# GpSimd makes twelve of the weights' low halves in a two-layer decoder trunk

## The chip, the cores and the metric

The kernel runs on one core of a Trainium2 chip. The metric is the device time of one execution in microseconds (us). The time before is the median of three runs. All times of instructions come from one profiled execution of the kernel before.

## What is computed

A decoder trunk of two layers on one sequence of 256 tokens with 1024 features, in float32:

```python
def reference(x, ...):
    h = x
    for i in range(DEPTH):                       # 2 layers
        hn = rmsnorm(h, mix_norm_g[i])
        if i % N_MIXERS == 0:
            mix = gated_deltanet(hn, ...)        # layer 0, 8 heads of 128, chunkwise delta rule
        else:
            mix = moba_layer(hn, ...)            # layer 1, block attention with ALiBi
        h = h + mix.astype(h.dtype)
        h = h + squared_relu_mlp(rmsnorm(h, mlp_norm_g[i]), mlp_w_up[i], mlp_w_down[i])
    return rmsnorm(h, final_norm_g)
```

The work is mostly products of the 256 tokens with weight matrices: 1024x4112 into the DeltaNet mixer and 1024x1024 out of it, 1024x3072 and 1024x1024 for the attention, and 1024x4096 and back for each of the two MLPs.

## The kernel before

All large weights are laid out by the host as a stream of 200 units. A unit is a tile of 128x1024 float32 (512 KB) and is used once, in order. To keep float32 accuracy on TensorE (PE) each float32 value is split into a high half that is rounded to the type float32r and a low half that is the rest, and a product is made of three matmuls: high times high, high times low, low times high (`mm3`, lines 128 to 133; `natural` and `mlp_last` write out the same three).

`prep(u)` (lines 105 to 117) prepares one unit. SyncE (SP) issues its DMA from HBM into `wf`, which has three buffers (line 114). ScalarE (ACT) copies `wf` to `wh`, which rounds (line 115). VectorE (DVE) subtracts, `wl = wf - wh` (line 116). `wh` and `wl` have five buffers each. The first eight units (`WHALF = 8`) go in two pieces of 512 columns each, the others in one. `unit()` (lines 121 to 126) hands out the next unit and first prepares all units up to four ahead (`LEAD = 4`).

Units 0 to 31 belong to the DeltaNet projections: 16 units for the q/k pairs of eight heads (`pair`, PSUM tile `ps_kq`), 8 for v (`ps_v`) and 8 for z (`natural`, `ps_z`), in the order of the string `ORDER`. Units 32 to 39 are the mixer's output projection (`ps_g`), and from unit 40 on follows the first MLP (`ps_up_m`, then `ps_dn_m`), the attention (`ps_qk`, `ps_vn`, `ps_a`) and the second MLP (`ps_up_m`, `ps_last`).

In the DeltaNet part VectorE has much beside L116: it scales each projection into `cin` (L478), adds three taps of the short convolution (L484, six per pair, from the SBUF tiles `cin` and `y`), multiplies the tanh form of silu (L510, `kq`, followed by PE's transposes `kqt` of L517), prepares the decay (L463, `ms`), scales the k and q products (L549, `ua`, from PSUM) and inverts the triangular matrices (L569 to L642). GpSimd only fills tiles with zeros: `cin` (L472), `xt` (L564) and `xy` (L565).

The kernel is written with Tile: the semaphores are put in by it, and the order on each engine is made by a planner that can depart from the order of the source. Each engine then runs its own instructions strictly in that order.

Of the kernel before, what the change touches and what calls it, by code (L numbers as in the profile page):

```python
# [7 lines left out]
F32 = mybir.dt.float32  # L8
# [17 lines left out]
LEAD = 4  # L26
WHALF = 8
WARM = 6
NLAST = 2
NTANH = 3  # L30
RS = 3.0 / 8
# [44 lines left out]
def trunk_kernel(ctx: ExitStack, tc: tile.TileContext, xT, wst, wba, par, con, selc, gfin, out):  # L76
    nc = tc.nc
# [8 lines left out]
    def bank(role, shape, name):  # L86
        tag = ROLE[role]
        return psum.tile(shape, F32, tag=tag, name=name, bufs=BANKS[tag])
# [16 lines left out]
    def prep(u):  # L105
        if u >= NUNIT or u in ring:
            return
        wf = wpool.tile([P, CW], F32, tag="wf", name=f"wf{u}", bufs=3)
        wh = wpool.tile([P, CW], F32R, tag="wh", name=f"wh{u}")
        wl = wpool.tile([P, CW], F32R, tag="wl", name=f"wl{u}")  # L110
        n = 2 if u < WHALF else 1
        for i in range(n):
            s = slice(i * CW // n, (i + 1) * CW // n)
            nc.sync.dma_start(wf[:, s], wst[u, :, s])
            nc.scalar.copy(wh[:, s], wf[:, s])  # L115
            nc.vector.tensor_sub(wl[:, s], wf[:, s], wh[:, s].bitcast(F32))  # L116
        ring[u] = (wh, wl)

    cur = [0]
# [1 line left out]
    def unit():  # L121
        u = cur[0]
        cur[0] += 1
        for i in range(u, u + LEAD + 1):
            prep(i)
        return ring[u]
# [8 lines left out]
    def mm(o, l, r, start=True, stop=True):  # L135
        nc.tensor.matmul(o, l, r, start=start, stop=stop, skip_group_check=True)  # L136
# [89 lines left out]
    def project_out(name, oh, ol, hin, nxt):  # L226

        pss = [bank("out" + "abcd"[i], [P, 2, T], f"ps_{name}_{i}") for i in range(4)]

        first = H - NLAST  # L230

# [129 lines left out]
    pw = bank("gate", [P, 512], "warm")  # L361
    for _ in range(WARM):
        mm(pw[:, :T], wu[:, 0, :P], wu[:, 0])
# [7 lines left out]
    for st in START.split():  # L371
        if st == "w":
            prep(nprep)
            nprep += 1
        elif st == "f":
            n0.feed(h0, nfeed)
            nfeed += 1
        else:
            queues[st[1]].dma_start(*loads[st[0]])
# [588 lines left out]
```

## Time and profile before

| | before |
|---|---|
| median of three runs | 649.35 us (648.83 to 649.79) |
| the profiled execution | 651.13 us |
| its span, first to last instruction | 649.3 us |
| granted TensorE clock, mean | 0.996 |
| PE busy | 634.4 us (98%) |
| VectorE busy | 453.7 us (70%) |
| ScalarE busy | 345.1 us (53%) |
| GpSimd busy | 4.0 us (1%) |
| L116, the low halves, on VectorE | 208 instructions, 244.3 us |

Busy time is time in which the engine has at least one instruction under way. Instructions of one engine overlap a little, so the start of the next one tells better than the length of a record how long an instruction keeps its queue. Idle time of an engine counts only if another engine, in the end PE, waits for it.

### The profile page before, as it was taken

What the parts mean: (1) busy time and instruction counts of PE and PEld (TensorE: products, weight loads), DVE (VectorE), ACT (ScalarE), POOL (GpSimd) and SP (SyncE); (2) the same over time, 40 slices, a digit from 0 to 9 for tenths busy, and PEclk for the clock granted to TensorE, in tenths of its full rate; (3) what the DMA queues carried; (4) which work ended last, traced back from release to release, by engine and by line L of the source; (5) the groups of instructions that cost most, each with busy time, mean ns of one, the idle gap of its engine ahead of it and who ended that gap; (6) DMA issues with size and microseconds to landing.
All of it is one profiled execution on the core that took longest, in us unless ns stands there. A gap on an engine that the chain in (4) does not pass through costs nothing.

```text
span 649.3 us, 13944 instructions
## 1 busy us (share of the span) xinstructions
PE 634.4 (98%) x5754; PEld 608.5 (94%) x5754; DVE 453.7 (70%) x841; ACT 345.1 (53%) x570; POOL 4.0 (1%) x10
## 2 busy tenths in 40 slices
PE   8999999999999999999999999999999999999995
PEld 6988887978999999999999999889999999999995
DVE  5999998997797666645554757775877776545443
ACT  6679873463566666634443444552656555434331
POOL 1000000000000000000000000000000000000000
PEclk9999999999999999999999999999999999999998
DMA  7754253252456565666565655555556666556641
GB/s 259 238 187 130 66 163 100 68 163 66 152 160 185 195 194 195 193 196 194 195 195 195 190 166 163 162 163 162 157 160 204 196 196 195 163 195 195 195 132 65
DMA packets 32031, 109.46 MB, mean 169 GB/s; under 512 B 3552, under 2 KB 3936, under 8 KB 31968
## 3 DMA queue, kind: packets, MB, share of 16 engines
q1 hardware_dynamic: 31248, 107.71, 52.5%
q8 instruction: 45, 0.74, 0.5%
q10 hardware_dynamic: 720, 0.86, 0.4%
q14 instruction: 18, 0.15, 0.1%
HBM read 107.51 MB, written 1.05 MB: 167 GB/s over the span
## 4 chain that ended last, share of the span: by engine, by line
PE 85%; DVE 5%; ACT 5%; DMA 4%; issue 1%; ACTq 0%; DVEq 0%
PE ps_last L136 12%; PE ps_up_m L132 8%; PE ps_up_m L133 8%; PE ps_up_m L130 8%; PE ps_dn_m L133 4%; PE ps_dn_m L132 4%; PE ps_dn_m L130 4%; PE ps_vn L136 3%; DMA wf<-in_w 3%; PE ps_z L136 3%; DVE wl L116 2%; PE ps_qk L132 2%; PE ps_qk L133 2%; PE ps_qk L130 2%; ACT wh L115 2%; PE kk L136 2%
## 5 line engine op out<-in xcount | busy, mean ns | idle before, releaser
L116 DVE TENSOR_TENSOR wl<-wf,wh 128x1024 fp32r<-128x1024 f32 (+1 forms) x208 | 244.3, 1182 | 141.0 <-ACT wh L115 140.4
L115 ACT CAST wh<-wf 128x1024 fp32r<-128x1024 f32 (+1 forms) x208 | 209.7, 1017 | 235.8 <-PE ps_up_m L132 63.7
L130 PE MATMUL ps_up_m<-n_h,wh 128*128 128x256 f32 x512 | 141.6, 277 | 0.5 <-ACT n_h L169 0.5
L132 PE MATMUL ps_up_m<-n_l,wh 128*128 128x256 f32 (+1 forms) x516 | 141.9, 276 | 0.0
L133 PE MATMUL ps_up_m<-n_h,wl 128*128 128x256 f32 x512 | 141.8, 277 | 0.0
L130 PEld LDWEIGHTS ps_up_m<-n_h,wh 128*128 128x128 f32 x512 | 96.1, 188 | 0.7 <-ACT n_h L169 0.7
L132 PEld LDWEIGHTS ps_up_m<-n_l,wh 128*128 128x128 f32 x516 | 96.6, 188 | 0.0
L133 PEld LDWEIGHTS ps_up_m<-n_h,wl 128*128 128x128 f32 x512 | 96.1, 188 | 0.0
L130 PE MATMUL ps_dn_m<-hh_m,wh 128*128 128x256 f32 x256 | 70.7, 276 | 0.0
L132 PE MATMUL ps_dn_m<-hl_m,wh 128*128 128x256 f32 x256 | 70.7, 276 | 0.0
L133 PE MATMUL ps_dn_m<-hh_m,wl 128*128 128x256 f32 x256 | 70.7, 276 | 0.0
L136 PE MATMUL ps_last<-wl,hh_m 128*128 128x256 f32 x226 | 61.9, 276 | 0.0
L136 PE MATMUL ps_last<-wh,hl_m 128*128 128x256 f32 x224 | 61.9, 276 | 0.0
L136 PE MATMUL ps_last<-wh,hh_m 128*128 128x256 f32 x224 | 61.8, 276 | 0.0
L130 PEld LDWEIGHTS ps_dn_m<-hh_m,wh 128*128 128x128 f32 x256 | 48.0, 188 | 0.0
L132 PEld LDWEIGHTS ps_dn_m<-hl_m,wh 128*128 128x128 f32 x256 | 48.0, 188 | 0.0
L133 PEld LDWEIGHTS ps_dn_m<-hh_m,wl 128*128 128x128 f32 x256 | 48.0, 188 | 0.0
L136 PEld LDWEIGHTS ps_last<-wl,hh_m 128*128 128x128 f32 x226 | 42.3, 188 | 0.0
L136 PEld LDWEIGHTS ps_last<-wh,hh_m 128*128 128x128 f32 x224 | 42.1, 188 | 0.0
L136 PEld LDWEIGHTS ps_last<-wh,hl_m 128*128 128x128 f32 x224 | 42.0, 188 | 0.0
L130 PE MATMUL ps_kq<-n_h,wh 128*128 128x256 f32 x128 | 36.6, 286 | 0.0
L130 PE MATMUL ps_qk<-n_h,wh 128*128 128x256 f32 x128 | 36.3, 284 | 0.0
(278 smaller groups left out, 1292.1 us busy)
## 6 DMA issues: line engine op xcount, KB each, us to landing
wf<-in_w SPq DMA_DIRECT2D x192, 512.0 KB, 3.5
wf<-in_w SPq DMA_DIRECT2D x16, 256.0 KB, 4.2
h<-in_x SPq DMA_DIRECT2D x4, 256.0 KB, 6.5
gf<-in_g SPq DMA_DIRECT2D x1, 512.0 KB, 4.0
out<-hg SPq DMA_DIRECT2D x2, 256.0 KB, 2.1
out<-hg ACTq DMA_DIRECT2D x2, 256.0 KB, 2.5
sel<-in_sel SPq DMA_DIRECT2D x1, 448.0 KB, 4.9
cn<-in_con SPq DMA_DIRECT2D x1, 276.0 KB, 4.9
```

What stands on the lines that cost most here:

```text
L115: nc.scalar.copy(wh[:, s], wf[:, s])
L116: nc.vector.tensor_sub(wl[:, s], wf[:, s], wh[:, s].bitcast(F32))
L130: nc.tensor.matmul(o, wh, xh, start=start, stop=False, skip_group_check=True)
L132: nc.tensor.matmul(o[:, s], wh, xl[:, s], start=False, stop=False, skip_group_check=True)
L133: nc.tensor.matmul(o, wl, xh, start=False, stop=stop, skip_group_check=True)
L136: nc.tensor.matmul(o, l, r, start=start, stop=stop, skip_group_check=True)
```

## The change

A constant `GEND = 44` is added. For units 8 to 43 whose number is a multiple of three (9, 12, 15, ..., 42: twelve units) the subtraction of line 116 is issued on GpSimd and no longer on VectorE. Its operands and its place in the source stay the same.

```diff
@@ -26,6 +26,7 @@
 LEAD = 4
 WHALF = 8
 WARM = 6
+GEND = 44
 NLAST = 2
 NTANH = 3
 RS = 3.0 / 8
@@ -113,7 +114,9 @@
             s = slice(i * CW // n, (i + 1) * CW // n)
             nc.sync.dma_start(wf[:, s], wst[u, :, s])
             nc.scalar.copy(wh[:, s], wf[:, s])
-            nc.vector.tensor_sub(wl[:, s], wf[:, s], wh[:, s].bitcast(F32))
+
+            e = nc.gpsimd if WHALF <= u < GEND and u % 3 == 0 else nc.vector
+            e.tensor_sub(wl[:, s], wf[:, s], wh[:, s].bitcast(F32))
         ring[u] = (wh, wl)
```

## Rows read from the trace of the kernel before

**Rows 1.** The page: engines' busy us, share, instructions; shares of the chain that ended last

```profile
PE 634.4 (98%) x5754; PEld 608.5 (94%) x5754; DVE 453.7 (70%) x841; ACT 345.1 (53%) x570; POOL 4.0 (1%) x10
...
PE 85%; DVE 5%; ACT 5%; DMA 4%; issue 1%; ACTq 0%; DVEq 0%
```

**Rows 2.** Timeline of VectorE: start us, length us, line, tiles, count

```profile
26.40 0.17 DVE L416 TENSOR_TENSOR gt_u<-ba,pm 128x16 f32<-128x16 f32 x1
26.48 0.48 DVE L484 SCALAR_TENSOR_TENSOR y_kq<-cin,pm,y_kq 128x256 f32<-128x256 f32 x1
...
31.05 1.21 DVE L116 TENSOR_TENSOR wl<-wf,wh 128x1024 fp32r<-128x1024 f32 x1
32.18 0.16 DVE L430 SCALAR_TENSOR_TENSOR gt_p<-gt_p,gt_z 128x16 f32<-128x16 f32 x1
32.27 0.41 DVE L510 SCALAR_TENSOR_TENSOR kq<-th,y_kq 128x256 f32<-128x256 f32 x1
...
82.91 1.22 DVE L116 TENSOR_TENSOR wl<-wf,wh 128x1024 fp32r<-128x1024 f32 x1
...
84.66 1.22 DVE L116 TENSOR_TENSOR wl<-wf,wh 128x1024 fp32r<-128x1024 f32 x1
...
177.65 1.23 DVE L116 TENSOR_TENSOR wl<-wf,wh 128x1024 fp32r<-128x1024 f32 x1 [1.63 <-ACT wh L115]
```

**Rows 3.** Busy us (instructions) by stretch: PE, PEld, DVE, ACT, POOL; clock, DMA share, GB/s

```profile
40.00:150.00 110.00, 108.26 (x1324) 93.32 (x1323) 103.92 (x288) 73.35 (x182) 1.05 (x2) 1.00 0.36 112
150.00:187.00 37.00, 36.22 (x309) 35.08 (x306) 28.54 (x67) 20.64 (x42) 0.00 (x0) 1.00 0.39 121
```

**Rows 4.** PE's waits from 20 to 200 us: us in total, times, longest

```profile
PE kqt L517 <- DVE kq L510: 1.6, 2, 0.8
PE ps_up_m L130 <- ACT n_h L169: 0.5, 1, 0.5
...
PE ps_z L136 <- DVE cin L478: 0.3, 1, 0.3
...
PE n_pb L136 <- DVE n_col L189: 0.2, 1, 0.2
```

**Rows 5.** GpSimd's groups by shape: busy us, mean ns, idle before

```profile
L564 POOL MEMSET xt<- 128x1024 f32 x2 | 1.8, 954 | 0.0
```

**Rows 6.** Timeline of GpSimd: start us, length us

```profile
44.79 0.53 POOL L565 MEMSET xy<- 64x512 f32 x1 [41.27 <-DVE kq L510]
57.69 0.52 POOL L565 MEMSET xy<- 64x512 f32 x1 [12.37 <-DVE kq L510]
```

**Rows 7.** Timeline of ScalarE, the copy of unit 21

```profile
73.50 1.05 ACT L115 CAST wh<-wf 128x1024 fp32r<-128x1024 f32 x1 [2.71 <-PE ps_v L132]
```

**Rows 8.** Timeline of PE: start us, length us, idle before in brackets

```profile
32.73 0.33 PE L517 MATMUL kqt<-cn,kq 128*128 128x128 f32 x1 [0.79 <-DVE kq L510]
...
84.40 0.40 PE L136 MATMUL ps_z<-wl,n_h 128*128 128x512 f32 x1
...
87.85 0.39 PE L136 MATMUL ps_z<-wl,n_h 128*128 128x512 f32 x1
```

**Rows 9.** Waits of SP's DMA queue over the span

```profile
SPq L114 <- DVE wl L116: 437.3, 165, 16.5
```

**Rows 10.** L463 on VectorE: ns min/median/max, first and last start

```profile
L463 DVE TENSOR_SCALAR ms<-cn,gt_gc x16: 270/278/623, 37.6 to 86.8; 128x128 f32<-128x128 f32 x16
```

**Rows 11.** Timeline of VectorE beside GpSimd's two fills

```profile
44.59 1.08 DVE L463 TENSOR_SCALAR ms<-cn,gt_gc 128x128 f32<-128x128 f32 x4
...
57.79 1.23 DVE L116 TENSOR_TENSOR wl<-wf,wh 128x1024 fp32r<-128x1024 f32 x1 [0.22 <-ACT wh L115]
```

**Rows 12.** VectorE's groups from 40 to 150 us: busy us, mean ns, idle before

```profile
L116 DVE TENSOR_TENSOR wl<-wf,wh 128x1024 fp32r<-128x1024 f32 x24 | 29.2, 1219 | 2.6 <-ACT wh L115 2.6
L484 DVE SCALAR_TENSOR_TENSOR y_kq<-cin,pm,y_kq 128x256 f32<-128x256 f32 x42 | 18.4, 478 | 0.0
L484 DVE SCALAR_TENSOR_TENSOR y_v<-cin,pm,y_v 128x256 f32<-128x256 f32 x24 | 11.2, 475 | 0.0
```

## The prediction

> **What bounds the kernel now.** I read the page's busy times, then its chain that ended last, then VectorE's timeline, three stretches of the windows view, and PE's waits. PE is busy for 634.4 of 649.3 us and carries 85% of the chain [rows 1]: the kernel ends when PE has issued its matmuls, and another engine matters only where it makes PE wait. The twelve moved subtractions are every third full-width row of L116, from unit 9 at 31.05 to unit 42 at 177.65, twelve by count [rows 2]. From 40 to 150 us, the DeltaNet part, VectorE is busy 103.92 us of 110 and PE 108.26; from 150 to 187 VectorE has 8.46 us free [rows 3]. So VectorE is a second full engine exactly where the change works. Yet between 20 and 200 us PE waits only 2.1 us in all on VectorE (1.6 on the q/k products, 0.3 on a convolution input, 0.2 on a norm), and the other four of the view's seven rows, the largest 0.5, add 1.3 [rows 4]. VectorE's load is hidden behind PE's, just. There are about 3 us to win, and 6 us of free VectorE time to lose.
>
> **What is removed.** A full-width L116 costs VectorE 1.13 us of queue time (31.05 to the next start at 32.18 [rows 2]; its record of 1.21 overlaps the next one). Twelve go: 12 x 1.13 = 13.6 us. Eight of them lie in the tight stretch (units 12 to 33, the first at its edge): 8 x 1.13 = 9.0 us. Unit 9 lies before it, units 36, 39 and 42 after it, where VectorE has slack.
>
> **What is added on GpSimd.** Twelve subtractions of 128x1024 with two inputs. The trace has no two-input operation on GpSimd; the nearest row is its fill of 128x1024, which only writes, in 0.954 us [rows 5]. Lower end: reading two streams while writing one costs no more than the fill, 0.95. Upper end: two reads and a write one after the other, 3 x 0.954 = 2.86. I take the two reads one after the other with the write beside them, 2 x 0.954 = 1.91 us, the value nearest to the row that still counts both inputs.
>
> The Trainium skill, "GPSIMD Engine Reference", section "3.1 Elementwise — side-by-side cycle accounting", gives 4497 ns for a two-input add of 2048 elements; an estimate from that page is 2.25 us for 1024. No run here shows it, and it lies inside the ends above.
>
> GpSimd's own queue holds little else: two fills at 44.79 and 57.69, the first after 41.3 us of waiting for VectorE [rows 6]. If the first were put ahead of unit 12's subtraction, that one would wait until 45.3 us; unit 12's weights are first used at about 53.6 by a count of PE's matmuls, so this is covered. Twelve times 2.86 is 34 us over 150: GpSimd cannot be the bound itself.
>
> **Is the weight itself late?** No. GpSimd can start when ScalarE's copy is done and need not stand in VectorE's queue. Unit 21: the copy starts at 73.50 and takes 1.05 [rows 7], VectorE's subtraction only starts at 84.66 [rows 2], and PE first needs it at 87.85 [rows 8]. GpSimd would be done by 77.5 even at 2.86. Unit 9 is done at 32.26 today [rows 2], and by the same count PE is first on it at about 39.9. If that cover were gone, each late unit would cost PE its lateness directly. The one weight that is nearly late, unit 20 (subtracted until 84.13, used at 84.40 [rows 2, 8]), is not moved. SP's DMA queue waits for L116 to free the three landing buffers, 437 us in all [rows 9], so the next thing to be late is a load. At unit 42, where VectorE waits for the copy today and starts at once when it is done (177.65 [rows 2]), the buffer comes free 0.7 us later at 1.91 and 1.6 later at 2.86; PE is more than 8 us behind the subtraction there by that count, so nothing is paid. No instruction is moved past another on SP.
>
> **Does VectorE keep what it is relieved of?** This decides. L463 takes 0.278 us at the median and 0.623 at most [rows 10]. The long one is in the group of four at 44.59 that took 1.08 us, and GpSimd's fill ran from 44.79 to 45.32 just there [rows 6, 11]. So VectorE's operation was held until GpSimd's had ended. Under the other fill (57.69 to 58.21) an L116 from 57.79 ran its usual 1.23 [rows 6, 11]. The hold depends on the forms, and the trace has none for a GpSimd operation that reads. Bounds for each moved subtraction: no hold, or the whole GpSimd operation less the time until the first VectorE operation that is held comes up (about 0.3 us, less than one L484 of 0.48).
>
> The Trainium skill, "SBUF — State Buffer", section "Who interferes with whom", says that a VectorE instruction with two SBUF inputs contends with a GpSimd instruction that reads SBUF, and that the loser waits for the whole instruction. The trace agrees in the part it can show (L463 held, L116 not held under a fill that reads nothing). By this rule and 2.25 us, 8 x 1.95 = 15.6 us would be held against 9.0 removed, VectorE would have 110.5 us of work for 110, and the time would be about 3.7 us longer.
>
> I take the full hold, because the one row that shows a hold shows it to the end of GpSimd's operation. It need not hit every form: VectorE runs in order, and L484 and the remaining L116, which like GpSimd's own operation read two SBUF tiles, are half of the stretch (29.6 us and about 19 of 103.92 [rows 3, 12]); the next of them stops L549 and the PSUM reads behind it. At 1.91: 8 x 1.61 = 12.9 us held, 9.0 removed, VectorE has 107.8 us of work. Packed without a gap this fits into 110 and costs nothing; packed as today (103.92 / 110 = 0.945) it needs 114.1, +4.1. I take the middle, +2.0 us. At 2.86: 20.5 held, 115.4 of work, +5.4 without a gap, +12 as packed today. At 0.95: 5.2 held, 100.1 of work, nothing lost, and at most PE's own 1.74 us of idle in the stretch won. Unit 9 and the three late ones add 4 x 0.5 us where VectorE has slack: nothing.
>
> **The order.** Instructions do not run in source order: L416, of the gates, stands among the first convolution's L484 [rows 2]. With twelve steps moved, a planner may place others differently. PE runs in order too: it stood 0.8 us twice before a transpose whose product was late [rows 4], the first time at 32.73 [rows 8], and unit 9's subtraction stands just ahead of that product, which starts at 32.27 [rows 2]. Such places can vanish or appear; two of them, 1.6 us either way, are the bound.
>
> **The rivals.** (A, the forecast) full hold: VectorE pays 1.6 us to save 1.13, is late by more than its gaps, and PE waits for transposes and products: +2.0 us, 651.35. It decides from a hold of 1.13 us on.
> (B) Little or no hold, below about 0.5 us each. VectorE falls to between 95 and 99 us in the stretch, the products come earlier, and PE's two waits of 0.8 us go: 647.75; at most all 3.4 us of the listed waits [rows 4]. For it: the L116 that ran under a fill. Against it: the held L463.
> (C) Hold and relief cancel, or VectorE's gaps take the rest: within 1.3 us of today, about 649.6. For it: PE hardly waits on VectorE now [rows 4].
> (D) The change does nothing, because GpSimd is itself kept waiting by VectorE until the relief is spent: the time is C's, and its chance is in C's.
>
> **How the numbers follow.** The profiled execution took 651.13 us, 649.3 of it the span; the median of the runs is 649.35, 1.8 lower, and I lay the difference on the median: 649.35 + 2.0 = 651.35 us. About 0.2%, 1.3 us, is what a measurement can tell from no change. A 0.45, of it 0.05 above 656; C and D 0.27; B 0.28, of it 0.08 below 647.4. So the range leaves out 0.13. It goes from 647.4 (B with a little more than its two waits) to 656.0 (the upper price without a gap, +5.4, and most of the 1.6 for the order). A's own range is 650.7 to 656. Faster 0.28, same 0.27, slower 0.45.
>
> **What would show it.** Right: twelve subtractions on GpSimd near 1.9 us; L484 or L116 rows beside them well over 0.48 and 1.23 that end with GpSimd's; VectorE's busy time above 103.9 us in the DeltaNet part; new PE waits on VectorE there. Wrong: L484 at 0.48 beside GpSimd and VectorE some 9 us lighter, which is B. GpSimd rows over 2.9 us, or PE waiting for a low half from GpSimd, would break the price or the cover.

## The result: 666.6 us, 2.5% slower, and the profile after

The changed kernel takes 666.58 us at the median (664.53 to 667.17), beside 649.52 of the kernel before (648.83 to 649.79): a ratio of 1.0252 [1.0237, 1.0267]. The forecast was 651.35 and its range ended at 656.0. So the direction was right, and the size was 17 us where the sum said 2. The profiled execution took 666.77 us, 664.9 of it the span. In the changed kernel the lines behind the edit stand three further down: L116 is L119, L484 is L487, L510 is L513 and L517 is L520; ScalarE's copy, L115, is L116 there.

From the page of the changed kernel: busy us, share of the span and instructions of each engine, the shares of the chain that ended last, PE's granted clock in 40 slices, and the moved subtractions.

```profile
PE 638.8 (96%) x5754; PEld 612.2 (92%) x5754; DVE 454.7 (68%) x829; ACT 347.8 (52%) x572; POOL 33.0 (5%) x22
...
PEclk9989979999999999999999999999999999999998
...
PE 81%; DVE 9%; ACT 4%; DMA 3%; issue 2%; ACTq 0%; DVEq 0%
...
L119 POOL TENSOR_TENSOR wl<-wf,wh 128x1024 fp32r<-128x1024 f32 x12 | 29.0, 2420 | 155.9 <-ACT wh L116 142.1
```

VectorE has twelve operations less and yet is busy 1.0 us longer than in [rows 1]. Its share of the chain goes from 5% to 9%.

The loss is all in one part. I measure the DeltaNet part from the first q/k matmul (`ps_kq`) to the first matmul of the MLP's up projection (`ps_up_m`): in the profiled executions it runs from 10.3 to 182.0 us before and from 9.4 to 197.6 after, 171.8 and 188.2 us. That is 16.4 us more, while what follows it is the same within 0.1 us (467.27 and 467.30) and what lies ahead of it was 0.9 shorter this time. Windows view, changed kernel: length, then busy us (instructions) of PE, PE's weight loads, VectorE, ScalarE and GpSimd, PE's granted clock, DMA share and GB/s.

```profile
9.40:197.60 188.20, 174.40 (x1835) 156.53 (x1834) 154.30 (x404) 112.04 (x259) 30.03 (x14) 0.97 0.39 126
40.00:150.00 110.00, 99.80 (x1192) 86.88 (x1191) 92.93 (x230) 67.72 (x161) 17.41 (x9) 0.95 0.31 101
43.90:45.90 2.00, 0.09 (x1) 0.09 (x2) 2.00 (x4) 1.56 (x2) 0.00 (x0) 0.99 0.45 184
45.90:49.30 3.40, 3.40 (x17) 3.34 (x18) 3.40 (x8) 2.07 (x12) 0.00 (x0) 0.50 0.48 154
81.10:83.40 2.30, 0.24 (x3) 0.04 (x1) 2.30 (x5) 0.00 (x0) 1.38 (x1) 1.00 0.00 0
83.40:90.20 6.80, 6.69 (x21) 5.71 (x22) 3.82 (x10) 3.23 (x9) 0.00 (x0) 0.50 0.52 154
```

The same view of the kernel before, over its DeltaNet part:

```profile
10.30:182.00 171.70, 168.88 (x1835) 152.38 (x1834) 153.75 (x418) 109.41 (x257) 1.05 (x2) 1.00 0.44 139
```

First row of the changed kernel: in the DeltaNet part PE is idle for 188.2 - 174.4 = 13.8 us. Before, it was idle for 171.70 - 168.88 = 2.8. That is +11.0 us. Second row, against the first of [rows 3]: in 110 us PE does 99.80 us of work for 108.26, and VectorE 92.93 for 103.92; both engines stand more. Last four rows of the changed kernel: PE stands almost still for 2.0 us from 43.9 and for 2.3 us from 81.1, and behind each of these its granted clock is 0.50 (1.2 GHz of 2.4), for 3.4 us and for 6.8 us. Before, the clock stood at its full level through the whole part. The 1,835 matmuls of the part keep PE busy for 174.40 us in place of 168.88, 5.5 us more, and 11.0 + 5.5 is the whole of the 16.4 us but for rounding. Most of the 5.5 lies in the two stretches at half clock: there neighbouring `ps_z` matmuls start 0.43 us apart, and 0.23 behind them (timeline of the changed kernel, first two and last two rows). So nearly half of 3.4 + 6.8 = 10.2 us is lost, an estimate of 4.7 us.

```profile
85.57 0.63 PE L139 MATMUL ps_z<-wh,n_l 128*128 128x512 f32 x1
86.00 0.63 PE L139 MATMUL ps_z<-wh,n_h 128*128 128x512 f32 x1
...
91.18 0.39 PE L139 MATMUL ps_z<-wl,n_h 128*128 128x512 f32 x1
91.41 0.39 PE L139 MATMUL ps_z<-wh,n_l 128*128 128x512 f32 x1
```

Timeline of the changed kernel around the second stand: start us, length us, operation, and in brackets the idle time before it and its releaser.

```profile
80.02 2.46 POOL L119 TENSOR_TENSOR wl<-wf,wh 128x1024 fp32r<-128x1024 f32 x1 [7.51 <-ACT wh L116]
...
80.17 2.59 DVE L487 SCALAR_TENSOR_TENSOR y_kq<-cin,pm,y_kq 128x256 f32<-128x256 f32 x1
82.69 0.16 DVE L584 TENSOR_TENSOR sm<-sb,uc 128x8 f32<-128x8 f32 x1
...
83.20 0.17 DVE L585 TENSOR_TENSOR xc<-xc,sm 128x8 f32<-128x8 f32 x1
...
81.06 0.28 PE L136 MATMUL ps_v<-n_h,wl 128*128 128x256 f32 x1
...
83.51 0.58 PE L139 MATMUL sb<-xc,sel 128*128 128x16 f32 x2 [2.17 <-DVE xc L585]
```

This is one hold in six rows. GpSimd starts at 80.02. The convolution step L487, usually 0.48 us, comes up on VectorE at 80.17 and ends at 82.76, 0.28 us behind GpSimd's end at 82.48. The tiny L584 and L585 stand behind it in VectorE's queue. PE's next matmul needs `xc` of L585 and waits 2.17 us; everything behind it in PE's queue waits too, though it needs nothing of it. It is not alone: over the whole part, L487 now reaches 2.6 us in both its uses (ns min/median/max, then first and last start); before, its longest was 0.49.

```profile
L487 DVE SCALAR_TENSOR_TENSOR y_kq<-cin,pm,y_kq x48: 393/476/2592, 25.7 to 92.3; 128x256 f32<-128x256 f32 x48
L487 DVE SCALAR_TENSOR_TENSOR y_v<-cin,pm,y_v x24: 467/478/2615, 94.5 to 160.0; 128x256 f32<-128x256 f32 x24
```

Going through VectorE's timeline beside each of the twelve, the operations under GpSimd were lengthened by 2.2, 1.9, 1.0, 0, 2.1, 2.1, 0, 2.0, 0.7, 0.6, 0 and 0.5 us, together some 13, against 13.6 us taken off. PE's waits between 20 and 220 us, the first four rows (us in total, times, longest; "issue" means that the profile shows nothing that PE waited for):

```profile
PE kqt L520 <- DVE kq L513: 5.8, 3, 2.7
PE sb L139 <- DVE xc L585: 3.8, 2, 2.2
PE py L139 <- DVE ss L527: 1.4, 1, 1.4
PE pd L139 <- issue: 1.2, 1, 1.2
```

In the kernel before [rows 4] the first of these was 1.6 us with 0.8 at the longest, and the other three were not there. No PE wait names GpSimd.

### The profile page after: what moved, and what is told of

Same layout as the page of the kernel before. It is cut to its first block, busy times and chain, and to the rows that moved or that the text cites. A ratio compares the mean times of both kernels' runs of the same rounds, so it can differ in the third digit from the quotient of the medians.

```text
span 664.9 us, 13964 instructions
## 1 busy us (share of the span) xinstructions
PE 638.8 (96%) x5754; PEld 612.2 (92%) x5754; DVE 454.7 (68%) x829; ACT 347.8 (52%) x572; POOL 33.0 (5%) x22
## 4 chain that ended last, share of the span: by engine, by line
PE 81%; DVE 9%; ACT 4%; DMA 3%; issue 2%; ACTq 0%; DVEq 0%
PE ps_last L139 11%; PE ps_up_m L135 8%; PE ps_up_m L133 8%; PE ps_up_m L136 8%; PE ps_dn_m L135 4%; PE ps_dn_m L136 4%; PE ps_dn_m L133 4%; PE ps_vn L139 3%; PE ps_z L139 3%; DVE wl L119 2%; PE ps_qk L135 2%; DMA wf<-in_w 2%; PE ps_qk L136 2%; PE ps_qk L133 2%; DVE y_kq L487 2%
## 5 line engine op out<-in xcount | busy, mean ns | idle before, releaser
L116 ACT CAST wh<-wf 128x1024 fp32r<-128x1024 f32 (+1 forms) x208 | 209.9, 1018 | 244.4 <-PE ps_up_m L135 63.9
L119 DVE TENSOR_TENSOR wl<-wf,wh 128x1024 fp32r<-128x1024 f32 (+1 forms) x196 | 229.7, 1179 | 141.6 <-ACT wh L116 140.8
L119 POOL TENSOR_TENSOR wl<-wf,wh 128x1024 fp32r<-128x1024 f32 x12 | 29.0, 2420 | 155.9 <-ACT wh L116 142.1
```

Of the source, the lines that this page charges most:

```text
L119: e.tensor_sub(wl[:, s], wf[:, s], wh[:, s].bitcast(F32))
```

## The experiments

The theory: GpSimd's two-input operation holds VectorE to its own end, and since PE runs in order, each hold is a delay at one place that PE pays at once, whatever VectorE saves elsewhere. The rivals: the new order that the planner writes (some 430 of PE's 5,754 matmuls stand at another place in the trace's order; 28 of the 32 transposes of L517 come earlier, most of them by 2 to 14 matmuls), a low half that is late, mere activity of GpSimd, or simply the sum of VectorE's work. Ratios are to runs of the kernel before on the same chip; the line numbers in these kernels' rows are those of before. The edits are shown in plain form, without the line that makes the scratch tile `junk_w`; where an edit takes up the changed kernel's line, it is shown against that one.

**The hold alone.** All of VectorE's instructions stay, and the order on PE, VectorE and ScalarE is that of before, instruction for instruction; GpSimd only does a subtraction of 832 columns more, into a tile that nobody reads.

```diff
             nc.vector.tensor_sub(wl[:, s], wf[:, s], wh[:, s].bitcast(F32))
+            (8 <= u < 44 and u % 3 == 0) and nc.gpsimd.tensor_sub(
+                junk_w, wf[:, :832], wh[:, :832].bitcast(F32))
```

> The kernel before with nothing taken off VectorE: for the same twelve units GpSimd makes, beside VectorE's subtraction, a second one of 832 columns into a scratch tile that nobody reads. The order of the instructions on PE, VectorE, ScalarE and SP is that of the kernel before, instruction for instruction. Theory H (the hold: a GpSimd subtraction stops VectorE's next operation that reads two SBUF tiles until it ends, VectorE is about 1.9 us late at once, and PE, which runs in order, stands): 8 to 18 us over the kernel before, L484 rows of over 1.5 us. Theory O (the order: the planner set PE's transposes earlier because it reckoned with a relieved VectorE): within 2 us of the kernel before, since the order is the old one.

Measured: 666.63 us, 1.025 [1.0222, 1.0278]. The DeltaNet part takes 187.7 us. GpSimd's group in this kernel (busy us, mean ns, idle before), then one place in its timeline, then the window of its DeltaNet part:

```profile
L116 POOL TENSOR_TENSOR junk_w<-wf,wh 128x832 f32<-128x832 f32 x12 | 27.1, 2260 | 159.4 <-ACT wh L115 159.4
```

```profile
99.96 2.01 POOL L116 TENSOR_TENSOR junk_w<-wf,wh 128x832 f32<-128x832 f32 x1 [17.09 <-ACT wh L115]
100.05 3.00 DVE L116 TENSOR_TENSOR wl<-wf,wh 128x1024 fp32r<-128x1024 f32 x1
```

```profile
9.40:197.10 187.70, 170.85 (x1836) 153.81 (x1835) 172.68 (x418) 109.85 (x257) 28.10 (x14) 0.99 0.41 126
```

A slowdown of the same size is there with no new order, no late weight and nothing moved: the operation on GpSimd alone is enough for it. A VectorE L116 under it takes 3.00 us for 1.22. Of the twelve places eleven are held by 1.6 to 1.8 us and one by 0.4, together 19.4 us, and with nothing taken off VectorE is busy for 172.68 us in place of 153.75. So this run shows that the hold is enough, but not whether its place or its sum counts: eight holds of 1.7 in the prediction's own formula, 103.9 + 13.6 = 117.5 us of work packed as before, would also give +14. In the changed kernel VectorE's sum did not grow; the equal totals of the two kernels are made up differently.

**Is it the reading?** The same place, three fills of 832 columns (some 2.4 us together) instead of the subtraction.

```diff
+            (8 <= u < 44 and u % 3 == 0) and [
+                nc.gpsimd.memset(junk_w, 0.0) for _ in range(3)]
```

> As the run before, but GpSimd fills the scratch tile three times (about 0.78 us each, 2.3 us together, by 0.954 us for 1024 columns) and reads nothing. Order on the other engines again that of the kernel before. Theory H: within 1.5 us of the kernel before, L116 and L484 at their usual 1.22 and 0.48 us, only forms like L463 held. Theory O: within 1.5 us as well. A third theory, that any work on GpSimd slows VectorE: as long as the extra subtractions.

Measured: 650.68, 0.9997 [0.9972, 1.0023]. GpSimd's group in this kernel, then two VectorE lines (ns min/median/max, first and last start):

```profile
L116 POOL MEMSET junk_w<- 128x832 f32 x36 | 28.6, 794 | 1.9
```

```profile
L116 DVE TENSOR_TENSOR wl<-wf,wh x208: 682/1226/1231, 4.5 to 630.8; 128x1024 fp32r<-128x1024 f32 x96, 128x512 fp32r<-128x512 f32 x8
...
L484 DVE SCALAR_TENSOR_TENSOR y_kq<-cin,pm,y_kq x48: 404/479/489, 26.1 to 83.1; 128x256 f32<-128x256 f32 x48
```

GpSimd is busy for as long as with the subtractions, 28.6 us, and no L116 or L484 is lengthened at all. The fills depend on nothing, so 34 of the 36 ran back to back between 4.9 and 33.8 us, not through the whole part; the second half of the test is the run with fills spread over the part, three further down.

**One input for two, in the changed kernel's order.** GpSimd copies the unit's values (a copy has one input) where it subtracted.

```diff
-            e = nc.gpsimd if ... else nc.vector
-            e.tensor_sub(wl[:, s], wf[:, s], wh[:, s].bitcast(F32))
+            if 8 <= u < 44 and u % 3 == 0:
+                nc.gpsimd.tensor_copy(wl[:, s], wf[:, s])
+            else:
+                nc.vector.tensor_sub(wl[:, s], wf[:, s], wh[:, s].bitcast(F32))
```

> The changed kernel, but on GpSimd a plain copy of the weights stands for the twelve subtractions (one input instead of two; the low halves of these units are then wrong, everything else is as in the change). The order on PE, VectorE, ScalarE and SP is that of the changed kernel, instruction for instruction. Theory H: the GpSimd operation is about 1 us (between 0.95 and 1.9), the hold is shorter in proportion, so at most half of the 17 us remains: 2 to 8 us over the kernel before. Theory O: still 13 to 17 us over it, because the order is the new one.

Measured: 654.14, 1.0076 [1.0045, 1.0106]. The DeltaNet part takes 175.6 us, PE is idle for 5.8 of it, and its clock stays at its full level. PE's longest wait in this kernel, and its longest L484:

```profile
PE kqt L517 <- DVE kq L510: 1.6, 1, 1.6
```

```profile
L484 DVE SCALAR_TENSOR_TENSOR y_v<-cin,pm,y_v x24: 470/480/1172, 85.8 to 148.1; 128x256 f32<-128x256 f32 x24
```

In the same order, with the operation on GpSimd at 1.04 us at the median (1.23 on average) in place of 2.42, five VectorE operations are held, by 0.7 to 0.9 us, 3.9 us together for some 13, and 12.4 of the 17 us are gone. So most of the loss comes with the two-input operation and not with the order. Length and place are not told apart here: the copy need not wait for ScalarE and starts earlier, unit 15's at 47.64 us in place of 52.95.

**The same subtraction in eight pieces.** Each of the twelve becomes eight of 128 columns, in the changed kernel's order.

```diff
+                for c in [slice(k * 128, (k + 1) * 128) for k in range(8)]:
+                    nc.gpsimd.tensor_sub(wl[:, c], wf[:, c], wh[:, c].bitcast(F32))
```

> The changed kernel with each of GpSimd's twelve subtractions cut into eight pieces of 128 columns, same result, same total work for GpSimd (12 x 2.4 us and some overhead). Order on the other engines that of the changed kernel. Theory H with a hold that ends with each piece: VectorE gets in between two pieces, so a held operation waits some 0.3 to 0.5 us and not 2.1; 3 to 10 us over the kernel before. Theory H with a hold that passes from piece to piece: 15 us or more over it. Theory O: 13 to 17 us over it.

Measured: 664.49, 1.0226 [1.0188, 1.0263]: 14.1 us over the kernel before, so hardly any help. The profiled execution was the fastest of the four, 662.15. Timeline of this kernel (x8 and x6 are rows of several operations), and PE's wait on the products:

```profile
41.57 5.55 POOL L116 TENSOR_TENSOR wl<-wf,wh 128x128 fp32r<-128x128 f32 x8 [7.81 <-ACT wh L115]
...
41.94 3.48 DVE L484 SCALAR_TENSOR_TENSOR y_kq<-cin,pm,y_kq 128x256 f32<-128x256 f32 x6 [0.19 <-ACT y_kq L482]
```

```profile
PE kqt L517 <- DVE kq L510: 5.6, 3, 3.6
```

The long hold is gone, but the two engines now take turns: eight pieces of 0.46 us (3.7 by themselves) stretch to 5.55 us, and six L484, 2.45 us where nothing holds them (the changed kernel at 46.02), take 3.48. VectorE pays some 9 us in pieces of 0.1 to 0.3 us where it paid 13 in long ones; GpSimd too is kept waiting. This suggests that the time counts for which the two want the same thing, and not only the longest single hold. The 14.1 us lie between the first two ranges expected and inside that of the order; against the order speak the extra subtraction (old order, +16) and the copy (this order, +4.6).

**Relief and new order without the hold.** GpSimd fills the twelve low halves with zeros and reads nothing; VectorE is relieved of its twelve subtractions.

```diff
+            if 8 <= u < 44 and u % 3 == 0:
+                nc.gpsimd.memset(wl[:, s].bitcast(F32), 0.0)
```

> The relief without a reading GpSimd: the twelve subtractions leave VectorE, and GpSimd only fills these low halves with zeros (0.95 us each, no input; the low halves of these units are wrong, all else as before). VectorE is 13.6 us lighter, the order on PE is not that of either kernel but near the changed one. Theory H (the hold is the cause, relief is worth little because PE hardly waited on VectorE): from 3 us under the kernel before to 1 us over it. Theory O (the new order costs by itself): 4 us over the kernel before or more.

Measured: 653.51, 1.0073 [1.0040, 1.0107], between the two ranges expected; the longest L116 and L484 are 1.23 and 0.49 us, so neither is held, though seven L484 ran partly or wholly beside a fill. GpSimd's group in this kernel, the one form that a fill clearly held (L463, 0.81 us at most for 0.28), PE's two longest waits in the part, and the timeline around the longest:

```profile
L116 POOL MEMSET wl<- 128x1024 f32 x12 | 11.5, 961 | 155.3 <-PE ps_v L133 47.3 <-PE ps_kq L133 44.2 <-PE ps_z L136 33.3
```

```profile
L463 DVE TENSOR_SCALAR ms<-cn,gt_gc x16: 277/280/810, 36.7 to 87.9; 128x128 f32<-128x128 f32 x16
```

```profile
PE kqt L517 <- DVE kq L510: 2.5, 2, 2.2
PE pd L136 <- issue: 1.2, 1, 1.2
```

```profile
32.23 0.43 DVE L510 SCALAR_TENSOR_TENSOR kq<-th,y_kq 128x256 f32<-128x256 f32 x1 [1.10 <-ACT th L508]
...
32.71 0.33 PE L517 MATMUL kqt<-cn,kq 128*128 128x128 f32 x1 [2.22 <-DVE kq L510]
```

VectorE has 13.6 us less to do, is held for about 1 us in all, and the kernel is 3 us slower, not faster. In its DeltaNet part PE is idle for 5.6 us, 2.7 more than before. The wait at the first transpose is longer (2.22 us for 0.79 in [rows 8]), although the product is there at the same time, about 32.7: PE's part began 0.7 us earlier in this execution, the new order has PE at the transpose four matmuls, some 0.5 us, earlier, and VectorE itself waits 1.10 us for ScalarE's `th`. The second place is the 1.2 us in the middle of the `pd` matmuls, where the kernel before had 0.12; the changed kernel and the run with the copy have the same 1.2 there. So the relief together with the order that comes with it is worth nothing in this part and costs some us. The relief in the old order was not run.

**Holds in another place.** The edit at units 45 to 78, which are prepared ahead of and in the first MLP.

```diff
-            e = nc.gpsimd if WHALF <= u < GEND and u % 3 == 0 else nc.vector
+            e = nc.gpsimd if 44 <= u < 80 and u % 3 == 0 else nc.vector
```

> The same change at twelve units of the first MLP (units 45 to 78, every third) and none before: as many GpSimd subtractions of 2.4 us, where VectorE is busy for about 62% and its results are used late. The order on PE differs in eight lines from the kernel before. Theory H with its second part (a held VectorE costs only where PE needs its results within the hold): within 1.5 us of the kernel before although L116 and L267 are held as long. A theory by which each hold costs about its length wherever it falls: 12 us over it or more.

Measured: 655.43 (651.42 to 656.59), 1.0071 [1.0049, 1.0093], outside what I had expected. The profiled execution was the fastest of the eight, so its trace shows only a part; in it one hold, of the norm's last step at 186 us, costs PE 1.8 us:

```profile
PE ps_up_m L132 <- DVE n_l L170: 1.8, 1, 1.8
```

The other executions are 2 to 5 us longer. Their mean granted clock is 0.991 to 0.995, for 0.998 in the profiled one, and by these shares a lower clock is worth 2 to 4.6 us (an estimate); where in the execution it fell, no trace shows.

To separate the place from the edit, the extra subtraction of the first experiment went to units 54 to 87, which fall within the MLP, with the order of before.

```diff
+            (52 <= u < 88 and u % 3 == 0) and nc.gpsimd.tensor_sub(
+                junk_w, wf[:, :832], wh[:, :832].bitcast(F32))
```

> The extra subtractions of the first run (832 columns into a scratch tile, nothing relieved, order of PE, VectorE, ScalarE and SP that of the kernel before) at twelve units of the first MLP, 54 to 87 by threes, in place of the DeltaNet part. Place theory: VectorE is held as long (about 1.7 us each where it meets L116 or L267), but there its results are needed several us later, so PE does not wait and the time is within 1.5 us of the kernel before. Theory that each hold costs about its length wherever it falls: some 12 to 16 us over it.

Measured: 650.26, 0.9999 [0.9964, 1.0035]. GpSimd's group in this kernel, and the line that was held most:

```profile
L116 POOL TENSOR_TENSOR junk_w<-wf,wh 128x832 f32<-128x832 f32 x12 | 35.8, 2982 | 212.7 <-ACT wh L115 212.7
```

```profile
L267 DVE TENSOR_TENSOR hl_m<-sq_m,hh_m x32: 676/692/2444, 196.9 to 554.6; 128x512 fp32r<-128x512 f32 x32
```

Five operations are held as long as in the DeltaNet part (L267 takes 2.44 us for 0.69), the other seven by 0.2 to 0.6 us, together 10.6 us, and from 205 to 310 us PE does not wait once. So a hold does not cost its length wherever it falls. A hold is only a delay; the reading is that PE pays it where the held chain is due at once, and not where results are made ahead. VectorE also has idle time in the MLP (in the kernel before it is busy 74.14 of the 115 us from 195), and this run does not tell the two apart. GpSimd's rows of 2.98 us, for 2.26 in the first experiment, show that the wait goes both ways: it was kept behind VectorE's running L116.

**Is the price in proportion?** A shorter extra operation (a copy of 832 columns, 0.88 us, twelve times), and the extra subtraction for six units only, both in the order of before.

```diff
+            (8 <= u < 44 and u % 3 == 0) and nc.gpsimd.tensor_copy(junk_w, wf[:, :832])
```

> As the extra subtractions of the first run, order of the kernel before, nothing relieved, but GpSimd copies 832 columns of the weights (one input, about 0.85 us by the 1.04 us measured for 1024) into the scratch tile. Theory H, cost in proportion to the time held: twelve holds of some 0.6 us, 3 to 7 us over the kernel before, about as the changed kernel with a copy (4 to 5 us over), whose order and relief then play no part. Theory O: no change, since the order is the old one, and the 4 to 5 us of the run with a copy came from the order.

Measured: 651.80, 1.0022 [0.9999, 1.0045], below what I had expected.

```diff
+            (8 <= u < 44 and u % 6 == 0) and nc.gpsimd.tensor_sub(
+                junk_w, wf[:, :832], wh[:, :832].bitcast(F32))
```

> The extra subtractions of the first run at six units in place of twelve (12, 18, 24, 30, 36, 42). Order of the kernel before. Theory H: the cost goes with the number of holds, about half of 16 us, 6 to 10 us over the kernel before. If one or two places make up the cost (a single hold of PE and its clock), it is either under 4 or over 12 us.

Measured: 657.02, 1.0109 [1.0092, 1.0125]; PE is idle for 8.8 us in the DeltaNet part and its clock stays full. Six long ones, which hold VectorE for 9.1 us together, cost 7 us, and twelve, which hold it for 19.4, cost 16; the twelve copies, at 0.39 of the length, hold it for 4.3 and cost 1.4, not 6. The price goes about with the time held by the long ones. That most of a short one is taken up by slack is a guess: the copies wait only for the load and so fall in other places.

**Which of the twelve?** The change for two units only, and for the other ten.

```diff
-            e = nc.gpsimd if WHALF <= u < GEND and u % 3 == 0 else nc.vector
+            e = nc.gpsimd if u in (9, 12) else nc.vector
```

> The change for units 9 and 12 alone; the planner's order is its own again. In the changed kernel PE stood 2.7 and some 2 us before the transposes L520 just after these two, and the clock was at half for 3.4 us behind the second. If the cost sits at such places: 4 to 9 us over the kernel before, for 2 of 12 units. If it is spread evenly over the units: under 3.5 us.

Measured: 656.26, 1.0092 [1.0068, 1.0117]. Two units make more than a third of the loss: unit 9 among them, which my sum had put at nothing since VectorE has slack there. PE's wait on the products in this kernel, and the windows of its two stands, each with the stretch behind it:

```profile
PE kqt L517 <- DVE kq L510: 4.0, 2, 2.1
```

```profile
31.50:34.00 2.50, 0.65 (x6) 0.66 (x7) 2.50 (x8) 0.31 (x1) 0.75 (x1) 1.00 0.16 36
34.00:37.40 3.40, 3.40 (x19) 3.40 (x18) 1.76 (x7) 2.21 (x8) 0.00 (x0) 0.50 0.97 384
45.00:47.70 2.70, 0.81 (x7) 0.63 (x7) 2.70 (x7) 1.56 (x2) 0.36 (x1) 1.00 0.55 164
47.70:51.10 3.40, 3.40 (x19) 3.40 (x17) 3.40 (x9) 3.15 (x15) 0.16 (x1) 0.50 0.36 145
```

Two waits of about 2 us at the transposes, and 3.4 us at half clock behind each, which lose nearly half of that, 1.6 each (an estimate as above): 4.0 + 3.1 = 7.1 us, less the 1.6 us that PE waited there before, is 5.5 of the measured 6.1. The holds are 2.2 us of L428 and 1.9 of an L484; 2.3 us were taken off, VectorE's busy time in the part grows by 2.7 (156.41 for 153.75), and the two waits by 2.4. So here the waits are about what the relief leaves of the holds, and the clock behind them makes the larger part of the loss.

```diff
+            e = nc.gpsimd if 15 <= u < 44 and u % 3 == 0 else nc.vector
```

> The change for the other ten units, 15 to 42. If the cost goes with the holds that meet VectorE (six of these ten in the changed kernel, 8.6 us held together) and with the stretch at half clock behind unit 21: 6 to 12 us over the kernel before. If the first two made nearly all of it: under 4 us.

Measured: 659.74 us in one execution, and 669.84 to 670.22 in the three others, the profiled one among them. In the trace of that one the granted clock is 0.50 for 6.8 us from 113.0 and for 13.7 us from 154.0, behind PE waits of 1.4 and 1.9 us, and PE is busy for 178.5 us of the part, 9.6 more than before. The one shorter execution, 9.6 us over the kernel before, would fit the range expected, but a single one settles no price, so that of the ten is left open.

## Why the prediction was right in direction and wrong in size

**Right: the bound and the cover.** VectorE turned out to be the engine that decides, through PE's waits in the DeltaNet part; the rest of the execution did not move. No PE wait names GpSimd or a late low half, so the cover that was counted for the weights holds. The loads cost nothing that shows: no PE wait in the part names a weight's load, and the rest is equal within 0.1 us.

**Right: the full hold.** The row behind it was one L463 of 0.62 us beside a fill. The hold is real, it goes to the end of GpSimd's operation or a little beyond, and it hits L484, L116 and others. As the prediction put it, it does not hit every form: beside the subtraction at 70.12 VectorE was at work on L552, which reads PSUM, and lost nothing; timeline of the changed kernel:

```profile
70.12 2.39 POOL L119 TENSOR_TENSOR wl<-wf,wh 128x1024 fp32r<-128x1024 f32 x1 [7.50 <-ACT wh L116]
70.11 2.60 DVE L552 SCALAR_TENSOR_TENSOR ua<-kk,p,dx 128x256 f32<-128x256 f32 x6
72.63 0.48 DVE L487 SCALAR_TENSOR_TENSOR y_kq<-cin,pm,y_kq 128x256 f32<-128x256 f32 x1
```

The rule of the Trainium skill that the prediction weighed ("SBUF — State Buffer", section "Who interferes with whom") has GpSimd's reads contend with a VectorE instruction that takes two inputs from SBUF, and neither a pure write nor a PSUM operand do so. The traces agree for the subtractions (L487 2.59 us, L552 not lengthened) and for the fills beside L116 (1.23 us at most). That rule does not cover all that was held: L463, whose row the prediction counts as agreeing, has one full input and was held by fills that read nothing (0.62 us before, 0.81 in the run with fills), and L431, also with one, took 2.34 us under a subtraction. So L463 spoke for the length of a hold, and not for that rule.

**Mis-sized: the price on GpSimd.** 1.91 us was taken, 2.42 was measured (12 for 29.0 us). The bounds of 0.95 and 2.86 held it. The estimate from the Trainium skill ("GPSIMD Engine Reference", section "3.1 Elementwise — side-by-side cycle accounting"), 2.25 us, was nearer than mine. With 2.42 in the prediction's own formula, 8 x (2.42 - 0.3) - 9.0 = 8.0 us more work on VectorE in 110 us, or 111.9: +1.9 us without a gap and, at 0.945, +8.4. The middle would have been +5, not +17, so the price is not the main failure. The range's upper end, too, took the upper price without a gap and left out the +12 that the prediction itself had for it as packed today.

**Failed: "Packed without a gap this fits into 110 and costs nothing ... I take the middle, +2.0 us."** This step booked holds and relief in one account, VectorE's work, and asked whether the sum fits. The profile shows that the account was balanced: 13.6 us taken off, some 13 held, VectorE's busy time over the DeltaNet part 153.75 before and 154.30 after. By that account the kernel should have come out where rival C put it, at no change. It lost 16.4 us. Nor did the work pack more closely: from 40 to 150 us VectorE was busy for 92.93 / 110 = 0.845 of the time, for 0.945 before, and over the part it stood idle for 33.9 us in place of 17.9. The sign that the prediction asked for, VectorE above 103.9 us there, did not come. The two sides are not the same coin. A hold of 2 us comes at one place, in front of whatever stands in VectorE's queue, and PE, in order, stands at the first matmul that needs it. The relief comes as 1.13 us at another place, where PE was not waiting. The run with the fills shows the relief with its order and almost no hold: 13.6 us of VectorE's time gone, and no gain. The run with the extra subtraction shows the hold without relief or new order: +16.2 us, though there VectorE's busy time grew by 18.9 as well. The changed kernel itself tells place from sum: VectorE's busy time is even, and PE is idle for 11.0 us more, most of it at waits with a name. The same mistake put unit 9 at nothing "where VectorE has slack": slack of an engine is no cover for a chain that is due at once. In the run with two units the wait behind unit 9's hold grew from 0.8 to 2.1 us, with 3.4 us at half clock behind it, and the two units cost 6.1 us.

**Missing: PE's clock.** The prediction has no term for it. Several stands of some 2 us are followed in these traces by stretches at half clock, though not all; by the estimates above they are 4.7 of the 16.4 us in the changed kernel and about 3 of 6.1 in the run with two units. It is a follow-up cost of the same waits, and varies from run to run.

**Too small: the order.** Its bound was 1.6 us either way. The run with fills, in an order like the changed kernel's and with almost nothing held, is 3.2 us slower than the kernel before, the wait at the first transpose grew from 0.79 to 2.22 us (about half of that because the part began earlier), and a wait of 1.2 us among the `pd` matmuls is new. So the order, with the relief in it, comes out at some 3 us and not 1.6, against the change. How much of the changed kernel's own loss it is stays open: in the copy run (+4.6 in exactly the changed kernel's order) it cannot be told from the short holds, and the extra subtraction reaches the whole +16 without it, so the parts do not simply add.

**Also open.** Why the eighths, with no long hold, keep nearly the whole loss is read from rows (the pieces and L484 take turns), but it was not measured apart from the extra cost of eight instructions for one. Where the slower executions of the edit in the MLP lose their 2 to 5 us is not shown beyond their lower mean clock. A version with the operation on GpSimd placed only beside PSUM reads, which by the trace would cost nothing, was not tried; with a relief that is worth nothing here it has little to win.

## What to carry to other kernels

Don't balance a relief against a hold in one engine's busy time: ask for each place which operation is held, who stands behind it in order, and when PE needs it; in these runs a hold cost up to its full length where the result was due at once (2.1 us of hold at 80.17 in the changed kernel, a wait of 2.17), and nothing in an MLP where results are made ahead. Before work is moved to GpSimd beside a busy VectorE, a run that only adds GpSimd's operation, into a scratch tile, prices the hold with every order unchanged. And if an engine is 95% busy but PE hardly waits for it, expect from taking work off it at most those waits; here they were 3.4 us, and nothing was won.

## What the runs showed of the hardware

A two-input subtraction of 128x1024 on GpSimd takes 2.35 to 2.46 us in eleven of its twelve rows and 2.72 in the first, a one-input copy 1.04 at the median, a fill 0.96. The subtraction starts beside a running VectorE operation; an L487 that comes up next then ends some 0.28 us behind it (82.76 for 82.48 above). This befell also a tiny operation with one tensor input, L431 on 128x16 (timeline of the changed kernel), which is what delayed the product of the first transpose:

```profile
29.57 2.72 POOL L119 TENSOR_TENSOR wl<-wf,wh 128x1024 fp32r<-128x1024 f32 x1 [26.05 <-ACT wh L116]
29.98 2.34 DVE L431 TENSOR_SCALAR gt_p<-gt_z 128x16 f32<-128x16 f32 x1
...
33.39 0.33 PE L520 MATMUL kqt<-cn,kq 128*128 128x128 f32 x1 [2.72 <-DVE kq L513]
```

In the kernel before it took 0.16 us (there it is L428); here it is 2.34. PE then stood for 2.72 us, the longest wait of the part, and this one was not followed by half clock, while the stands of 2.0 and 2.3 us at 43.9 and 81.1 were. A wait thus cost its own length and, in these executions, at times about as much again behind it.
